# Stick-breaking attention: scores as two products over all 128 array rows, values padded to 128 columns

## The chip, the cores and the metric

One Trainium2 chip, one core of it. The metric is device time in microseconds (us) of one execution of the whole program; less is better. TensorE (PE in the profile) does the matmuls and loads their weights (PEld), VectorE is DVE, ScalarE is ACT, GpSimd is POOL, and SyncE (SP) issues the loads.

## The reference, cut to what matters

The program runs three transformer blocks in a row over 512 tokens of 1024 features. The change lies in the second one's mixer, stick-breaking attention with 16 heads of 64 dimensions:

```
z = einsum('bqhd,bkhd->bhqk', q_blk, k) * 64 ** -0.5
earlier = key_pos < q_pos
log_keep = where(earlier, log_sigmoid(-z), 0)
log_after = cumsum(log_keep over keys, reverse=True) - log_keep
weight = where(earlier, exp(log_sigmoid(z) + log_after), 0)
out = einsum('bhqk,bkhd->bqhd', weight, v)
```

The projections to q, k, v before it and the projection `w_out` after it belong to the same stage of the kernel. Everything is float32 in the reference. The kernel writes a float32 operand as the sum of a high part and a low part of a shorter type (F32R, `fp32r` in the profile) and adds products of parts: high by high, high by low and low by high.

## The kernel before, in words

`build` (L2064) runs the blocks one after the other: `block1`, `stick` (L601), `ffn`, `diff`, `ffn`. This change touches `stick` alone.

**Order.** `Driver` (L97) merges streams of work into one order of TensorE's instructions, by estimated microseconds (`mm`, L293, adds an estimate for each matmul) and by events that the streams set and wait for. The tile framework then orders the instructions of every engine by priority and by its own model of when operands are there. So a matmul stands in a fixed order in TensorE's queue, and a late operand holds what is behind it.

**Projections** (`projections`, L609). For each pair of heads `hp` (8 pairs) q and k are each one 128-feature chunk on all 512 tokens: 8 chunks of features by 3 products of parts, 24 matmuls of 512 columns. `evac_qk` (L610) multiplies the result by the norm's factor (DVE, L614), writes the high part on ACT (L615) and the low part on DVE (L616). Head 0 of the pair lies on partitions 0 to 63, head 1 on 64 to 127. For every second pair a group `g` of 256 columns of v (four heads) is projected with tokens on partitions; `scale_tm` (L571, L575) scales the result on ACT. The first pair and group are done side by side (`first_qk`, `first_v`), and their results wait for the norm's factors.

**Units** (`unit`, L664). One head's scores have keys on partitions and queries on columns, and only queries not before the key tile: key tile i has 512 - 128 i columns. They lie in three PSUM banks: tile 0, tile 1, and tiles 2 and 3 together. A unit is one bank of one head, so there are 48 units. Its steps: the score products and the mask into a bank `z` (5 banks); ACT does Abs, Exp and Ln (L686 to L688); DVE forms the softplus (L689) and splits it into `sh` and `sl` (L319, L320); TensorE adds the sums over later keys to the same bank, with the weights `negones` and `m_ntri`; ACT takes Exp into `w` (L705); TensorE multiplies `w` with v into the bank `po`, of which there is one. When both heads of a pair are through, `po` is split into `ohi` and `olo`, the operands of `w_out`.

The score products of one key tile take rows `d` of the array, the head's 64 partitions:

```
d = slice(64 * s, 64 * s + 64)
self.mm(zz, k[0][d, ks], q[0][d, P * i:], j == 0, False)
self.mm(zz, k[0][d, ks], q[1][d, P * i:], False, False)
self.mm(zz, k[1][d, ks], q[0][d, P * i:], False, False)
self.mm(zz[:, :P], self.neg30, self.m_ge, False, False)
```

The fourth, the mask, has all 128 rows and 128 columns. The product with v (L717) is in float32, not in parts; its weights are v's 64 columns of the head, and its output goes to the 64 partitions `d` of `po`. One float32 matmul stands in the trace as two records.

**Memory.** Tiles of 128 x 512 float32 come from one pool of 57 chunks (`big`), and scratch from a pool of 9 (`tmp`). A tile's place is free again after its last reader.

In the trace, `64*128` ahead of a matmul's shape means that its weights have 64 rows and 128 columns, and `128*64` that they have 128 rows and 64 columns.

Of the kernel before, what the change touches and what calls it, by code (L numbers as in the profile page):

```python
# [9 lines left out]
F32 = mybir.dt.float32  # L10
# [7 lines left out]
P = 128  # L18
T = 512
# [39 lines left out]
# 500000 ** (-j / 8) as float32 has it  # L59
# [5 lines left out]
def two_pi_parts():  # L65
    """2 pi as parts of 8, 12 and 24 bits"""
    rest, parts = 2 * math.pi, []
    for bits in (8, 12, 24):
        e = math.floor(math.log2(rest)) + 1 - bits
        part = math.floor(rest / 2.0 ** e) * 2.0 ** e if bits < 24 else rest  # L70
        parts.append(part)
        rest -= part
    return parts
# [11 lines left out]
class Slots:  # L85
    """free places of a resource, each with the time from which it is free"""
# [4 lines left out]
class Take:  # L91
    """n places of Slots at once"""
# [4 lines left out]
class Driver:  # L97
    """Merges the streams of work into one order of the tensor engine's instructions.

    A stream is a generator; it yields the microseconds until its next step's operands are there, an  # L100
    Event to wait for, or Slots of which it takes one."""
# [10 lines left out]
    def spawn(self, g):  # L112
        """one more stream, ahead of the others"""
        self.tasks.insert(0, [g, self.t, None])
# [38 lines left out]
class Raw:  # L153
    """x g of a norm as two parts, without the norm's factor 1/sqrt(mean of squares + eps) of the tokens; it
    goes on the results of the projections: r has it with the tokens on the free axis, rt on partitions"""
# [12 lines left out]
class Net:  # L168
    def __init__(self, ctx, tc, ins, out):
# [7 lines left out]
        # weights of the next proj_multi  # L177
# [3 lines left out]
        # the results of projections wait for this event  # L181
# [25 lines left out]
    def phase(self, name, **sizes):  # L207
        """pools of one part of the kernel"""
# [22 lines left out]
    def take(self, n):  # L231
        """counts n chunks as used"""
        self.mem.free.sort()
        del self.mem.free[:n]

    def drop(self, n, lat=0.0):
        """n chunks are read for the last time by what is issued now"""
        self.drv.release(self.mem, lat, n)
# [8 lines left out]
    def cmask(self, name, cmp, mult, base, val, dt=F32R):  # L247
        """val where base + mult*p + (-mult)*j  cmp 0, else 0"""
# [9 lines left out]
    def consts(self):  # L258
# [5 lines left out]
        # rows 0..63: 1, the others 0  # L264
# [7 lines left out]
        # [p, j]: 1 where p >= j, p <= j, p > j, p < j  # L272
# [4 lines left out]
        # columns 0..15 of the rows 16..31 of every 32  # L277
# [3 lines left out]
        # p - 32 b >= 16 and p - 32 b < 32, b by block of columns: one of the four is the row's own  # L281
# [40 lines left out]
    def wtile(self, ap, n=1024):  # L322
        """weights of one tile: [128, n] from DRAM, as two parts"""
# [11 lines left out]
    def wtile_big(self, ap):  # L335
        """weights [128, 1024] in chunks of 512 columns"""
# [12 lines left out]
    def evacuate(self, f, kind, lat, staged):  # L349
        """reads a bank, as soon as the norm's factors are there; a staged f only copies the bank, and returns the  # L350
        stream of the rest"""
# [12 lines left out]
    def proj_fm(self, w, h, evac, name, evs=None, lat=2.0, staged=False):  # L364
        """out[128 features, T] of one output chunk; w: (ap, k chunks) parts; evac(psum) reads the result"""
# [15 lines left out]
    def proj_tm(self, aps, h, evac, name, lat=2.0, evs=None, staged=False):  # L381
        """256 columns, tokens on partitions: evac(b, [128, 2 token tiles x 256]) for b = 0, 1"""
# [28 lines left out]
    def proj_halves(self, ap, h, evac, name):  # L411
        """the last output chunk before a norm, in two halves of the tokens: evac(psum, columns of the half)"""
# [12 lines left out]
    def proj_multi(self, items, h, name, evs, weights=None):  # L425
        """output chunks side by side, for operands that come slowly, with the weights in chunks of the big pool;
        items: (weights, evac(psum)) of a chunk of features, or ((weights, weights), evac(b, psum)) of 256 columns
        with tokens on partitions; at most 4 banks in all; the evacs are staged"""
# [35 lines left out]
    def out_proj(self, ws, h, evac, evs, late=1, last=None):  # L464
        """8 output chunks; the last `late` k chunks of the first two come after all their others"""
# [28 lines left out]
    def add_square(self, run, x):  # L494
        """run + x^2; run is None at the first"""
# [8 lines left out]
    def preload_ln(self):  # L504
        """the table of Ln and Exp, for the next norm"""
# [3 lines left out]
    def norm_sum(self, sums, cs):  # L509
        """sums over all features, on all partitions"""  # L510
# [5 lines left out]
    def rstd_of(self, sums, eps4=False, out=None, cs=slice(0, T), ps=None):  # L516
        """1/sqrt(mean of squares + eps) on all partitions, of the tokens cs; the squares' sums over the features of
        a partition are in sums, or ps has the sums over all"""
# [16 lines left out]
        # one Newton step: r (1.5 - 0.5 ms r^2)  # L535
# [35 lines left out]
    def scale_tm(self, out, ps, rt, b):  # L571
        """out = ps rt of the token tiles 2 b, 2 b + 1"""
# [19 lines left out]
    def add_to(self, x, R):  # L592
        """adds a projection to x; R, if any, takes the sum"""
# [7 lines left out]
    def stick(self, x, R, l, nxt, pre):  # L601
# [7 lines left out]
        def projections():  # L609
            def evac_qk(hp, wn, sc, ps):  # L610
                hi = self.chunk(wn + "hi", F32R)
                lo = self.chunk(wn + "lo", F32R)
                t = self.work("qk")
                nc.vector.tensor_tensor(t, ps, self.rfm, op=ALU.mult)  # L614
                nc.scalar.mul(hi, t, sc)  # L615
                nc.vector.scalar_tensor_tensor(out=lo, in0=t, scalar=sc, in1=hi.bitcast(F32),  # L616
                                               op0=ALU.mult, op1=ALU.subtract)
                qk[hp, wn] = (hi, lo)

            def evac_v(g, b, ps):  # L620
                t = v[g, b] = self.chunk(f"v{b}")
                self.scale_tm(t, ps, self.rt, b)
# [3 lines left out]
            def first_v(b, ps):  # L626
                t = v[0, b] = self.chunk(f"v{b}")
                nc.vector.tensor_copy(t, ps)

                def rest():  # L630
                    self.scale_tm(t, t, self.rt, b)
# [32 lines left out]
        def unit(hp, s, b, me, prev, head, pair):  # L664
            d = slice(64 * s, 64 * s + 64)
            # the key tiles of this bank: (tile, first column)
# [3 lines left out]
            hcol = 64 * ((2 * hp + s) % 4)  # L670
# [4 lines left out]
            q, k = qk[hp, "sb_q"], qk[hp, "sb_k"]  # L675
            z = self.bank("z", f"z{b}")
            for j, (i, c0) in enumerate(its):
                ks = slice(P * i, P * i + P)
                zz = z[:, c0:c0 + T - P * i]
                self.mm(zz, k[0][d, ks], q[0][d, P * i:], j == 0, False)  # L680
                self.mm(zz, k[0][d, ks], q[1][d, P * i:], False, False)
                self.mm(zz, k[1][d, ks], q[0][d, P * i:], False, False)
# [32 lines left out]
            for i, c0 in reversed(its):  # L715
                vt = v[g, i // 2][:, (i % 2) * 256 + hcol:(i % 2) * 256 + hcol + 64]
                self.mm(po[d, P * i:], vt, w[:, c0:c0 + T - P * i], i == 3, i == 0)  # L717
# [22 lines left out]
    def gates(self, R):  # L740
        """beta and the decays of the delta rule, tokens on partitions: columns (direction, chunk, head)"""
# [62 lines left out]
    def conv(self, ps, j, out, raw_h):  # L804
        """out = 2 silu(5-tap convolution along the tokens); ps: the channel's 512 tokens"""
# [18 lines left out]
    def silu2(self, out, ps, rt, b):  # L824
        """2 silu, without its factor rt"""
# [12 lines left out]
    def dn_prep(self, S, hh):  # L838
        """operands of one head of the batch S"""
# [6 lines left out]
        for x, w in enumerate("kq"):  # L846
            yield S["ev", w, hh]
            if w == "k":
                # kt, vt, U and two of aT
# [28 lines left out]
        # decays between the tokens of a chunk, both directions  # L878
# [35 lines left out]
        for w in "kq":  # L914
# [5 lines left out]
            if w == "k":  # L920
                # U of direction 0 is strictly upper, that of direction 1 strictly lower: one tile has both
# [17 lines left out]
    def dn_inv(self, S):  # L939
        """Y = (1 + U)^-1 of every head, direction and chunk of the batch: the diagonal blocks of 32 by  # L940
        substitution, one block per partition, then blocks of 64 and 128 on the tensor engine.
# [1222 lines left out]
```

## Time and profile before

| | |
|---|---|
| median of 3 runs | 2264.87 us |
| the three runs | 2253.7, 2264.87, 2268.81 us |
| span of the profiled execution, first to last instruction | 2268.6 us |
| PE busy | 2210.7 us (97%) |
| DVE busy | 1212.9 us (53%) |
| ACT busy | 963.9 us (42%) |
| POOL busy | 95.5 us (4%) |
| mean granted TensorE clock | 0.965 |

The profiled execution's own time is not listed apart from its span; the span is within 0.3 us of the slowest of the three runs. The stick-breaking stage lies between 907 and 1187 us of the span. "Busy" for PE means that a matmul was in the pipeline; it does not say how fast matmuls followed each other. The pace is read from the starts of successive matmuls in the timeline. The granted clock is 1.00 at the 2.4 GHz level and 0.50 at the 1.2 GHz level.

### The profile page before, as it was taken

To read this page: it belongs to the slowest core of one execution; us is meant where nothing else is said; L and a number is where in the kernel's file an instruction comes from. 1 tells how busy PE (TensorE), PEld (TensorE's weight loads), DVE (VectorE), ACT (ScalarE), POOL (GpSimd) and SP (SyncE) were. 2 spreads that over 40 slices of the span, in tenths; PEclk is the share of its full clock that TensorE was granted. 3 is DMA by queue.
4 is the path that set the end of the run, shared out by engine and by line. 5 is a ranking of instruction groups with operands and counts; after the bars stand their busy time and mean duration, and the time that the engine had idled before them with its cause. 6 is when DMAs were issued, how large, how long until landed. Compare 5 with 4: busy or idle time off the path is not lost.

```text
span 2268.6 us, 33416 instructions
## 1 busy us (share of the span) xinstructions
PE 2210.7 (97%) x13342; PEld 1855.4 (82%) x13342; DVE 1212.9 (53%) x2487; ACT 963.9 (42%) x1951; POOL 95.5 (4%) x109
## 2 busy tenths in 40 slices
PE   7999999989999998999999999999999999999999
PEld 6898898878888787777778888888999878888887
DVE  7865865976424567443346444433566656444421
ACT  5646666565423454544444223222444444232221
POOL 2000100000000000000000000000111100000000
PEclk9999999999999998899989999999898889999999
DMA  4221211323243521011103232233211113322332
GB/s 162 63 72 48 64 52 57 91 60 100 79 149 120 184 92 38 28 47 47 47 19 103 94 102 93 90 101 98 66 57 40 36 38 103 102 93 94 97 112 70
DMA packets 73995, 181.72 MB, mean 80 GB/s; under 512 B 24176, under 2 KB 24816, under 8 KB 73840
## 3 DMA queue, kind: packets, MB, share of 16 engines
q1 hardware_dynamic: 72560, 175.40, 24.2%
q0 software_dynamic: 1280, 4.20, 0.6%
q8 instruction: 105, 1.72, 0.3%
q14 instruction: 50, 0.41, 0.1%
HBM read 170.13 MB, written 9.44 MB: 79 GB/s over the span
## 4 chain that ended last, share of the span: by engine, by line
PE 84%; DVE 8%; ACT 3%; issue 1%; POOL 1%; DMA 1%; SPq 0%; DVEq 0%; ACTq 0%; POOLq 0%
PE pg L301 16%; PE pd L301 11%; PE pu L301 11%; PE po L301 9%; PE z L301 5%; PE pv L301 4%; PE pb L301 4%; PE s L301 3%; PE pz L301 2%; PE pq L301 2%; PE sb_q L301 2%; PE pk L301 2%; PE sb_k L301 2%; PE wS L301 2%; DVE cacc L818 1%
## 5 line engine op out<-in xcount | busy, mean ns | idle before, releaser
L317 ACT CAST whi<-st 128x1024 fp32r<-128x1024 f32 (+1 forms) x295 | 306.0, 1039 | 791.4 <-issue 340.3
L320 DVE TENSOR_TENSOR wlo<-st,whi 128x1024 fp32r<-128x1024 f32 (+1 forms) x295 | 355.9, 1208 | 284.8 <-ACT whi L317 280.9
L301 PE MATMUL pg<-rlo,whi 128*128 128x512 f32 x352 | 138.8, 394 | 0.0
L301 PE MATMUL pg<-rhi,whi 128*128 128x512 f32 x352 | 138.1, 392 | 0.0
L301 PE MATMUL pg<-rhi,wlo 128*128 128x512 f32 x352 | 138.0, 392 | 0.0
L301 PE MATMUL pd<-mh,whi 128*128 128x512 f32 x352 | 137.6, 391 | 0.0
L301 PE MATMUL pd<-mh,wlo 128*128 128x512 f32 x352 | 137.6, 391 | 0.0
L301 PE MATMUL pd<-ml,whi 128*128 128x512 f32 x352 | 137.5, 391 | 0.0
L301 PE MATMUL pu<-rhi,wlo 128*128 128x512 f32 x352 | 137.2, 390 | 0.0
L301 PE MATMUL pu<-rlo,whi 128*128 128x512 f32 x352 | 137.1, 390 | 0.0
L301 PE MATMUL pu<-rhi,whi 128*128 128x512 f32 x352 | 137.0, 389 | 0.0
L2032 DVE TENSOR_TENSOR sg<-pg,rfm 128x512 f32<-128x512 f32 x44 | 30.4, 691 | 118.5 <-PE pg L301 118.4
L2038 DVE TENSOR_TENSOR m<-pu,sg 128x512 f32<-128x512 f32 x44 | 30.4, 691 | 115.2 <-PE pu L301 115.2
L689 DVE SCALAR_TENSOR_TENSOR t<-z,t 128x384 f32<-128x384 f32 (+1 forms) x48 | 28.2, 600 | 99.8 <-ACT t L688 97.6
L301 PEld LDWEIGHTS pg<-rhi,wlo 128*128 128x128 f32 x352 | 66.2, 188 | 15.1 <-issue 0.5
L301 PEld LDWEIGHTS pg<-rlo,whi 128*128 128x128 f32 x352 | 66.3, 188 | 15.0 <-issue 0.5
L301 PEld LDWEIGHTS pg<-rhi,whi 128*128 128x128 f32 x352 | 66.2, 188 | 14.5
L301 PEld LDWEIGHTS pd<-ml,whi 128*128 128x128 f32 x352 | 66.2, 188 | 14.3
L301 PEld LDWEIGHTS pd<-mh,wlo 128*128 128x128 f32 x352 | 66.1, 188 | 14.3
L301 PEld LDWEIGHTS pd<-mh,whi 128*128 128x128 f32 x352 | 66.1, 188 | 14.2
L301 PEld LDWEIGHTS pu<-rhi,whi 128*128 128x128 f32 x352 | 66.1, 188 | 14.0
L301 PEld LDWEIGHTS pu<-rlo,whi 128*128 128x128 f32 x352 | 66.1, 188 | 14.0
(554 smaller groups left out, 5943.5 us busy)
## 6 DMA issues: line engine op xcount, KB each, us to landing
st<-w_gate SPq DMA_DIRECT2D x44, 512.0 KB, 3.4
st<-w_up SPq DMA_DIRECT2D x44, 512.0 KB, 3.4
st<-w_down SPq DMA_DIRECT2D x32, 512.0 KB, 3.5
st<-w_dn SPq DMA_DIRECT2D x24, 512.0 KB, 3.6
st<-w_out SPq DMA_DIRECT2D x24, 512.0 KB, 3.5
st<-w_down SPq DMA_DIRECT2D x16, 384.0 KB, 3.1
x<-xT SPq DMA_DIRECT2D x16, 256.0 KB, 5.9
st<-w_aq SPq DMA_DIRECT2D x8, 512.0 KB, 3.5
```

Source lines behind the costliest of these rows:

```text
L301: self.nc.tensor.matmul(out, lhsT=lhsT, rhs=rhs, start=start, stop=stop, skip_group_check=True)
L317: nc.scalar.copy(hi, src)
L320: nc.vector.tensor_tensor(lo, src, hi.bitcast(F32), op=ALU.subtract)
L689: nc.vector.scalar_tensor_tensor(out=t, in0=zz, scalar=0.0, in1=t, op0=ALU.max, op1=ALU.add)
L818: nc.vector.scalar_tensor_tensor(out=acc[:, a], in0=raw[:, b], scalar=w[:, s:s + 1], in1=acc[:, a], op0=ALU.mult, op1=ALU.add)
L2032: nc.vector.tensor_tensor(sg, ps, self.rfm, op=ALU.mult)
L2038: nc.vector.tensor_tensor(m, ps, sg, op=ALU.mult)
```

## The change

The score operands are stacked on partitions. For each head `stack` makes one query tile with the high part of q on the head's own 64 partitions and the low part on the other 64, and two key tiles: one with the high part of k on both halves, one with the low part of k on the own half and zeros on the other. Two products over 128 rows then give the three products of parts of before (the fourth term, of the zeros, adds nothing). The values are written with 64 columns of zeros beside each head's 64, so that the product with v has 128 columns of weights, writes all 128 partitions of `po`, and the two heads of a pair add up in one accumulation. Comments and docstrings are removed throughout; this is left out here.

```
+    def stack(self, box, j, query, src, sc):
+        nc = self.nc
+        for s in range(2):
+            own, other = slice(64 * s, 64 * s + 64), slice(64 - 64 * s, 128 - 64 * s)
+            f = sc if isinstance(sc, float) else sc[own]
+            x = src[own]
+            hi = self.chunk("qs" if query else "kh", F32R)
+            nc.scalar.mul(hi[own], x, f)
+            if query:
+                lo = hi[other]
+                box[j, "q", s] = hi
+            else:
+                t = self.chunk("kl", F32R)
+                nc.gpsimd.memset(t[other].bitcast(F32), 0.0)
+                lo = t[own]
+                box[j, "kh", s], box[j, "kl", s] = hi, t
+            nc.vector.scalar_tensor_tensor(out=lo, in0=x, scalar=f, in1=hi[own].bitcast(F32),
+                                           op0=ALU.mult, op1=ALU.subtract)
+            if not query:
+                nc.scalar.mul(hi[other], x, f)
...
             def evac_qk(hp, wn, sc, ps):
-                hi = self.chunk(wn + "hi", F32R)
-                lo = self.chunk(wn + "lo", F32R)
                 t = self.work("qk")
                 nc.vector.tensor_tensor(t, ps, self.rfm, op=ALU.mult)
-                nc.scalar.mul(hi, t, sc)
-                nc.vector.scalar_tensor_tensor(out=lo, in0=t, scalar=sc, in1=hi.bitcast(F32),
-                                               op0=ALU.mult, op1=ALU.subtract)
-                qk[hp, wn] = (hi, lo)
+                self.stack(qk, hp, wn == "sb_q", t, sc)
+
+            def pad_v(g, b, ps):
+                for i in range(2):
+                    t = v[g, 2 * b + i] = self.chunk(f"v{2 * b + i}")
+                    nc.gpsimd.memset(t.rearrange("p (a k) -> p a k", a=2)[:, :, 64:192], 0.0)
+                    nc.scalar.mul(t.rearrange("p (a k d) -> p a k d", a=2, k=4)[:, :, 0::3],
+                                  ps[:, i * 256:(i + 1) * 256].rearrange("p (a k d) -> p a k d", a=2, k=2),
+                                  self.rt[:, 2 * b + i:2 * b + i + 1])
 
             def evac_v(g, b, ps):
-                t = v[g, b] = self.chunk(f"v{b}")
-                self.scale_tm(t, ps, self.rt, b)
+                pad_v(g, b, ps)
...
             def first_v(b, ps):
-                t = v[0, b] = self.chunk(f"v{b}")
+                t = self.work(f"v{b}raw")
                 nc.vector.tensor_copy(t, ps)
...
-                    self.scale_tm(t, t, self.rt, b)
+                    pad_v(0, b, t)
...
-            hcol = 64 * ((2 * hp + s) % 4)
+            hcol = 128 * ((2 * hp + s) % 4)
...
-                self.mm(zz, k[0][d, ks], q[0][d, P * i:], j == 0, False)
-                self.mm(zz, k[0][d, ks], q[1][d, P * i:], False, False)
-                self.mm(zz, k[1][d, ks], q[0][d, P * i:], False, False)
+                self.mm(zz, kh[:, ks], q[:, P * i:], j == 0, False)
+                self.mm(zz, kl[:, ks], q[:, P * i:], False, False)
                 self.mm(zz[:, :P], self.neg30, self.m_ge, False, False)
...
-                vt = v[g, i // 2][:, (i % 2) * 256 + hcol:(i % 2) * 256 + hcol + 64]
-                self.mm(po[d, P * i:], vt, w[:, c0:c0 + T - P * i], i == 3, i == 0)
+                self.mm(po[:, P * i:], v[g, i][:, hcol:hcol + P], w[:, c0:c0 + T - P * i], s == 0 and i == 3, s == 1 and i == 0)
```

## Rows read from the trace of the kernel before

**Rows 1.** The page: busy us, share of the span and instructions by engine.
```profile
PE 2210.7 (97%) x13342; PEld 1855.4 (82%) x13342; DVE 1212.9 (53%) x2487; ACT 963.9 (42%) x1951; POOL 95.5 (4%) x109
```

**Rows 2.** Windows: stretch, length, busy us (instructions) by engine, clock, DMA share, GB/s.
```profile
907.00:1187.00 280.00, 280.00 (x1331) 211.53 (x1331) 116.19 (x197) 129.43 (x243) 0.00 (x0) 0.90 0.12 38
126.00:355.00 229.00, 221.69 (x2413) 202.50 (x2413) 145.88 (x376) 137.43 (x377) 14.40 (x12) 1.00 0.20 59
1645.00:1861.00 216.00, 215.19 (x1371) 189.16 (x1370) 132.59 (x465) 93.44 (x203) 26.73 (x19) 0.86 0.14 45
```

**Rows 3.** Timeline, one head's scores: start us, duration us, engine, line, operation, shapes.
```profile
976.61 0.39 PE L301 MATMUL sb_q<-rhi,wlo 128*128 128x512 f32 x1
976.92 0.38 PE L301 MATMUL z<-sb_qhi,sb_khi 64*128 64x256 f32 x1
...
977.26 0.27 PE L301 MATMUL z<-sb_qhi,sb_klo 64*128 64x256 f32 x1
977.47 0.33 PE L301 MATMUL z<-m_ge,neg 128*128 128x128 f32 x1
977.73 0.33 PE L301 MATMUL z<-sb_qhi,sb_khi 64*128 64x128 f32 x1
...
980.58 0.38 PE L301 MATMUL z<-sb_qhi,sb_khi 64*128 64x256 f32 x1
```

**Rows 4.** Timeline, the sums over later keys of one bank: full-array matmuls.
```profile
958.81 0.22 PE L301 MATMUL z<-sh,negones 128*128 128x128 f32 x1
958.87 0.28 PE L301 MATMUL z<-sl,negones 128*128 128x128 f32 x1
958.98 0.33 PE L301 MATMUL z<-sh,negones 128*128 128x256 f32 x1
...
960.07 0.28 PE L301 MATMUL pv<-whi,rhi 128*128 128x256 f32 x1
```

**Rows 5.** Timeline of the first block: a mask product with the same weights.
```profile
73.83 0.39 PE L301 MATMUL dec<-m_gt,neg 128*128 128x512 f32 x1
74.06 0.40 PE L301 MATMUL dk<-hlo,whi 128*128 128x512 f32 x1
```

**Rows 6.** Timeline: one product with v between projection matmuls.
```profile
961.62 0.40 PE L301 MATMUL sb_q<-rhi,wlo 128*128 128x512 f32 x1
961.94 1.07 PE L301 MATMUL po<-w,v 128*64 128x512 f32 x2
...
963.29 0.39 PE L301 MATMUL sb_q<-rlo,whi 128*128 128x512 f32 x1
```

**Rows 7.** Timeline: a float32 matmul of the full array between projection matmuls.
```profile
1226.78 1.10 PE L301 MATMUL nsum<-sq,ones 128*128 128x512 f32 x2
...
1227.94 0.39 PE L301 MATMUL pg<-rhi,wlo 128*128 128x512 f32 x1
```

**Rows 8.** Timeline: the first two of one pair's three runs with v, merged.
```profile
990.21 2.37 PE L301 MATMUL po<-w,v 128*64 128x128 f32 x8
...
995.36 1.51 PE L301 MATMUL po<-w,v 128*64 128x128 f32 x6
```

**Rows 9.** Windows: the stretch before a fall of the clock, and the stretch after.
```profile
979.20:982.60 3.40, 3.40 (x17) 2.49 (x16) 2.02 (x5) 3.40 (x8) 0.00 (x0) 1.00 0.00 0
...
982.70:986.10 3.40, 3.40 (x10) 2.58 (x9) 3.12 (x7) 2.15 (x6) 0.00 (x0) 0.50 0.00 0
```

**Rows 10.** Timeline at the lower clock: two successive projection matmuls.
```profile
983.75 0.63 PE L301 MATMUL sb_q<-rlo,whi 128*128 128x512 f32 x1
984.18 0.63 PE L301 MATMUL sb_q<-rhi,wlo 128*128 128x512 f32 x1
```

**Rows 11.** Groups by form: ACT and DVE in the stage, POOL in the span.
```profile
L615 ACT ACTIVATE sb_khi<-qk 128x512 fp32r<-128x512 f32 x8 | 5.0, 628 | 1.7 <-DVE qk L614 1.7
...
L616 DVE SCALAR_TENSOR_TENSOR sb_klo<-qk,sb_khi 128x512 fp32r<-128x512 f32 x8 | 5.5, 685 | 0.1
...
L1418 POOL MEMSET Y<- 128x512 f32 x4 | 1.9, 530 | 0.0
```

More of the change, by code (lines that the diff above doesn't have):

```diff
@@ L664, in unit @@
         def unit(hp, s, b, me, prev, head, pair):
-            d = slice(64 * s, 64 * s + 64)
             its = ((2, 0), (3, 256)) if b == 2 else ((b, 0),)
@@ L674, in unit @@
             yield self.free["z"]
-            q, k = qk[hp, "sb_q"], qk[hp, "sb_k"]
+            q, kh, kl = qk[hp, "q", s], qk[hp, "kh", s], qk[hp, "kl", s]
             z = self.bank("z", f"z{b}")
```

## The prediction

> **What bounds the kernel now.** I read the page first: TensorE is busy 97% of the span, VectorE 53%, ScalarE 42% [rows 1]. The windows view then gives the stage of the change, 907 to 1187 us [rows 2]: TensorE busy 280.00 of 280.00 us, ScalarE 129.43, VectorE 116.19, GpSimd nothing. So the stage lasts as long as TensorE's queue takes, and two things set that: how closely matmuls follow each other (starts in the timeline) and the granted clock. The clock's mean here is 0.90; in the first block's attention, whose products use the full array, it is 1.00, and in the differential attention, whose score products have 64 rows as here, 0.86 [rows 2].
>
> **Score products.** One head's scores are 12 products of 64 rows and 4 masks of 128 rows. They run from 976.92 to 980.58, 3.66 us at full clock [rows 3]. The columns alone do not explain it: the product ahead of a mask keeps the engine 0.21 us (977.26 to 977.47) for 256 columns, and the mask 0.26 us (977.47 to 977.73) for 128. That is a cost of the change of shape, paid twice per key tile. After the change everything here has 128 rows. A row for it exists: the sums over later keys of one bank are eight full-array matmuls of twice 128, 256, 384 and 512 columns, exactly the count and widths of one head's products after the change, and take 958.81 to 960.07, 1.26 us [rows 4]. A mask of 128 columns at full shape should take what 128 columns take there, 958.87 to 958.98, 0.11 us; and a mask with the same weights between full-array matmuls shows no extra, 0.23 us for 512 columns [rows 5]. Sum: 1.26 + 4 x 0.11 = 1.70 us. Saved: 1.96 us a head, **31.4 us** over 16 heads. Entering such a burst costs the matmul ahead 0.31 instead of 0.23 us (976.61 to 976.92 [rows 3]); at two bursts a pair, 16 x 0.08 = **1.3 us** more.
>
> **Product with v.** The pair of records at 961.94 stands between projection matmuls that otherwise follow every 0.23 us. From 961.62 + 0.23 to 963.29 - 0.23 it costs 1.21 us [rows 6]. A float32 matmul of the full array, also 512 columns and with 128 columns of weights to load, costs 1227.94 - 0.23 - 1226.78 = 0.93 us [rows 7]. So the padding itself costs nothing that shows, and a run of such products saves 0.28 us. A pair has three such runs in the timeline, of 8 and 6 records [rows 8] and one of 2 as in [rows 6]: 24 x 0.28 = **6.7 us**.
>
> **Clock.** Within the stage the clock falls eight times to 0.50, the 1.2 GHz level. What comes before is the same each time: a stretch of score products and masks (in one of the eight shared with products with v), with TensorE busy throughout (3.40 of 3.40 us) and still at 1.00, the 2.4 GHz level; then 0.50 [rows 9]. At that level a projection matmul of 512 columns takes 0.43 us instead of 0.23 [rows 10]. A mean of 0.90 over 280 us is 56 us at the lower level, which cost 56 x (1 - 0.23 / 0.43) = **26 us**. The first block's attention has the same pattern of three products, masks and float32 products with v, on full rows, and holds 1.00 for 229 us [rows 2]. So I take all 26 us as gained. The Trainium skill, TensorE: Matmul & The Clock Gate (Part 1), says that the gate follows how busy the engine has been. By busy time alone these falls should not occur, and full rows should not end them; the trace disagrees as long as "busy" means the PE row. With it the sum below would be 31 us and not 57, and the rule returns as a rival.
>
> **What is added.** Each pair's q and k cost ScalarE six scalings instead of two: 4 x 0.63 = 2.5 us a pair; VectorE four low parts instead of two: 2 x 0.69 = 1.4 us [rows 11]. No row has these forms on 64 partitions; I take them at the durations of 128, with the same 512 columns. Over 8 pairs that is 20 and 11 us. ScalarE then has about 149 us and VectorE 127 in a stage of some 215: 70% and 59%. Beneath: nothing, because ScalarE is idle 151 of these 280 us and VectorE 164 [rows 2]. Above: all 31 us on the path. I take 1 us a pair, **8 us**, near the lower end: TensorE has the next pair's projections between the steps of a pair, but the scores now come in about half the time, so ScalarE's three activations per bank are more often what is last. The first head of a pair needs one scaling and one low part for q and for k, as before; the second head's come while the first's products run.
>
> GpSimd gets 32 memsets, 16 of 64 x 512 and 16 of 128 x 256, at most 0.53 us each [rows 11], 17 us on an engine idle in this stage; behind them in its queue stands only the next norm's small power. A memset waits only for a free chunk, and the low part of k follows it. Cost nothing while a chunk is free ahead of the projection's end; without that cover, 0.53 us per memset. The scaling of v has the same count and width, with a strided output; nothing. The first v's raw copy moves from a chunk to scratch: nothing, since both are ready before the norm's factors. No DMA is added, removed or moved.
>
> **Sum.** 31.4 + 1.3 + 6.7 + 26 - 8 = 57 us. Against the profiled span: 2268.6 - 57 = 2211.6. The median of the runs stands 3.7 us below that span, so the forecast is 2264.87 - 57 = 2208, call it **2209 us**. Own range: all of the 65 us and the lowest run, 2253.7 - 65 = 2189, to 2222 with twice the stalls and a fall or two of the clock left.
>
> **Rivals.**
> (a) The clock still falls: the low activity comes from short matmuls and masks, or from something the half rows only go along with. For it: TensorE is already busy all through each stretch before a fall [rows 9], so "busy" does not explain them. Against: the first block [rows 2]. Time: 2209 + 26 = 2235. By the skill's rule named above, busy time would decide and this is what follows.
> (b) ScalarE and VectorE become the bound: all 31 us of their additions lie on the path instead of 8. For it: 70% of a stage with bursts. Against: 151 us of ScalarE's idle time to use up [rows 2]. Time: 2209 + 23 = 2232.
> (c) The delay belongs to the mask product, not to the change of shape: then only one product in three goes, 1.26 / 2 x 16 = 10 us instead of 33. Against: the mask in [rows 5]. Time: 2209 + 23 = 2232, and no more than one percent if (a) comes with it.
> (d) Slower: chunks run out. A pair's stacks are 6 chunks instead of 4, a group's values 4 instead of 2. Counted at the fifth finished pair with two pairs' stacks, two groups' values and both heads' sums alive: before 16 (the norm's output) + 8 + 4 + 12 + 10 (outputs) = 50 of 57; after 16 + 12 + 8 + 12 + 10 = 58, one too many. Then the next pair's q and k (48 matmuls x 0.23 = 11 us) have nowhere to go and no longer fill TensorE's time between the steps, which lie bare instead. It decides if it strikes more than 57 / 11, about 5 of the 7 later pairs; at all seven the time is 2209 + 77 = 2286, with the clock falling in the waits 2286 + 26 = 2312. Against: the maxima do not fall together; values of the older group end with the pair that the count has finishing, and one chunk too few is a short wait.
>
> **Chances.** Forecast 0.70, (a) 0.12, (b) 0.08, (c) 0.05, (d) 0.05. About 1%, 23 us, is what a measurement of this kernel can tell from no change: below 2242 is faster, above 2288 slower. Faster: 0.70 + 0.10 of (a) + 0.06 of (b) + 0.03 of (c) = 0.89; same: 0.07, where two of (a), (b), (c) meet; slower: 0.04, most of (d). The range runs from 2189 to 2243: it takes in the lone cases (a), (b), (c) and leaves out their meetings and (d).
>
> **What would show it.** Right: products of one head with their masks take about 1.7 us in the timeline, all `128*128`; the mask 0.11 us; the clock in the stage 0.98 or more; the stage some 57 us shorter; PE still busy over 97% of it. The stages before and after keep their length within a few us. Wrong: falls to 0.50 in the stage (a); PE idle with ACT as the releaser (b); masks still at 0.26 us (c); PE or POOL idle ahead of memsets or q and k evacuations, with projections bunched after a pair's last product with v (d).

## The result and the profile after

The changed kernel takes 2211.66 us, the median of 4 runs (2205.83 to 2215.02), against 2266.84 us for the kernel before, also 4 runs (2253.70 to 2274.84). The ratio is 0.9748, with a 95% interval from 0.9707 to 0.9789: faster by about 55 us. Forecast were 2209 us and a range of 2189 to 2243.

The page of the kernel after, busy time by engine and the granted clock in 40 slices of the span:
```profile
span 2213.2 us, 33421 instructions
...
PE 2152.9 (97%) x13278; PEld 1835.6 (83%) x13278; DVE 1222.8 (55%) x2503; ACT 980.7 (44%) x1983; POOL 108.9 (5%) x141
...
PEclk9999999999999998999999999999889889999999
```
Beside [rows 1]: TensorE still has 97%, of a span 55.4 us shorter; ScalarE and VectorE are busy 17 and 10 us longer, GpSimd 13. The page can't say where the 55 us were. For that I cut both traces at the same instructions: the stage runs from the first float32 sum of squares (`nsum`) of its norm to that of the next norm. The columns are those of [rows 2].

Windows of the kernel before: ahead of the stage, the stage, and from there to the last block's norm.
```profile
0.00:897.46 897.46, 845.68 (x6704) 737.42 (x6705) 575.16 (x1290) 475.57 (x1156) 59.19 (x83) 0.98 0.28 90
...
897.46:1226.78 329.32, 328.99 (x1541) 250.21 (x1540) 148.97 (x241) 154.42 (x280) 1.03 (x1) 0.92 0.14 44
...
1226.78:1905.64 678.86, 676.88 (x3532) 572.81 (x3531) 347.41 (x793) 242.42 (x405) 35.33 (x25) 0.94 0.24 76
```
The same windows of the kernel after:
```profile
0.00:904.32 904.32, 852.12 (x6705) 743.52 (x6705) 575.26 (x1290) 475.75 (x1156) 60.60 (x87) 0.97 0.28 90
...
904.32:1175.82 271.50, 269.18 (x1476) 227.30 (x1476) 158.67 (x257) 171.05 (x312) 12.99 (x29) 1.00 0.17 53
...
1175.82:1850.29 674.47, 672.47 (x3531) 569.76 (x3531) 347.50 (x793) 242.35 (x405) 35.33 (x25) 0.95 0.24 77
```
The stage went from 329.32 to 271.50 us, **57.8 us** less, and its clock from 0.92 (54.6 us of it at 0.50) to 1.00 (none). The stretch ahead, which the change does not touch, is 6.9 us longer at a lower clock (0.98, then 0.97), and the one behind 4.4 us shorter at a higher one; the rest is equal. 57.8 - 6.9 + 4.4 = 55.3 us, the difference of the spans. The 6.9 us are no cost of the change: in the kernels below, whose work ahead of the stage is the same, this stretch ends anywhere from 898.6 to 904.2 us.

Timeline of the kernel after, one head's scores (columns as in [rows 3]):
```profile
970.46 0.39 PE L301 MATMUL sb_q<-rhi,wlo 128*128 128x512 f32 x1
970.68 0.28 PE L301 MATMUL z<-qs,kh 128*128 128x256 f32 x1
970.80 0.28 PE L301 MATMUL z<-qs,kl 128*128 128x256 f32 x1
970.92 0.22 PE L301 MATMUL z<-m_ge,neg 128*128 128x128 f32 x1
970.98 0.27 PE L301 MATMUL z<-qs,kh 128*128 128x128 f32 x1
...
972.35 0.33 PE L301 MATMUL z<-qs,kh 128*128 128x256 f32 x1
...
1015.33 0.28 PE L301 MATMUL pv<-wlo,rhi 128*128 128x256 f32 x1
1015.45 1.02 PE L301 MATMUL po<-w,v 128*128 128x512 f32 x2
1015.91 0.79 PE L301 MATMUL sb_q<-rhi,whi 128*128 128x512 f32 x1
1016.54 0.39 PE L301 MATMUL sb_q<-rlo,whi 128*128 128x512 f32 x1
```
The head runs from 970.68 to 972.35, 1.67 us instead of 3.66 [rows 3]. The mask at 970.92 keeps the engine 0.06 us, and the product ahead of it 0.12, where before they kept it 0.26 and 0.21; the burst costs the matmul ahead of it 0.22 us, no more than any projection. The product with v at 1015.45 takes, to the second projection behind it less 0.23, 0.86 us instead of 1.21 [rows 6].

### The profile page after: what moved, and what is told of

Its sections match the earlier page's. It is cut to its first block, busy times and chain, and to the rows that moved or that the text cites. A ratio compares the mean times of both kernels' runs of the same rounds, so it can differ in the third digit from the quotient of the medians.

```text
span 2213.2 us, 33421 instructions
## 1 busy us (share of the span) xinstructions
PE 2152.9 (97%) x13278; PEld 1835.6 (83%) x13278; DVE 1222.8 (55%) x2503; ACT 980.7 (44%) x1983; POOL 108.9 (5%) x141
## 4 chain that ended last, share of the span: by engine, by line
PE 83%; DVE 9%; ACT 4%; issue 2%; POOL 1%; DMA 1%; SPq 0%; DVEq 0%; ACTq 0%; POOLq 0%
PE pg L301 17%; PE pd L301 11%; PE pu L301 11%; PE po L301 9%; PE pb L301 4%; PE pv L301 4%; PE s L301 3%; PE pz L301 3%; PE z L301 3%; PE pq L301 2%; PE pk L301 2%; PE wS L301 2%; PE sb_q L301 2%; DVE cacc L845 1%; PE sb_k L301 1%
## 5 line engine op out<-in xcount | busy, mean ns | idle before, releaser
L301 PE MATMUL pz<-wlo,hhi 128*128 128x256 f32 x256 | 75.2, 294 | 3.3 <-DVE wlo L320 2.5
```

The source lines that it names most:

```text
L301: self.nc.tensor.matmul(out, lhsT=lhsT, rhs=rhs, start=start, stop=stop, skip_group_check=True)
```

## The experiments

Each is an edit of one of the two kernels. "Stage" is the stretch between the two `nsum` records, "low" the time in it at a granted clock of 0.50. Ratios are to the kernel before, run on the same chip at the same time. The stage of e8 and e10 is that of the kernel after, unchanged: its three traces agree within 0.01 us.

| kernel | stage, us | low, us | ratio (95%) |
|---|---|---|---|
| before | 329.3 | 54.6 | |
| after | 271.5 | 0 | 0.9748 (0.9707 to 0.9789) |
| e1 scores only | 280.4 | 0 | 0.9801 (0.9773 to 0.9829) |
| e2 values only | 316.4 | 37.5 | 0.9940 (0.9911 to 0.9970) |
| e3 three full-row products | 279.2 | 0 | 0.9777 (0.9747 to 0.9807) |
| e4 before, no mask | 279.1 | 0 | 0.9763 (0.9732 to 0.9795) |
| e5 after, float32 mask | 278.3 | 0 | 0.9803 (0.9769 to 0.9837) |
| e6 the same in two halves | 296.6 | 0 | 0.9858 (0.9823 to 0.9893) |
| e7 ScalarE's additions doubled | 291.8 | 6.8 | 0.9852 (0.9817 to 0.9888) |
| e9 copy of k on GpSimd | 272.5 | 0 | 0.9755 (0.9716 to 0.9794) |
| e11 before, no mask, one half | 283.6 | 0 | 0.9804 (0.9739 to 0.9870) |
| e8 stack in `diff` too | 271.5 | 0 | 0.9613 (0.9580 to 0.9645) |
| e10 e8, later due time | 271.5 | 0 | 0.9619 (0.9565 to 0.9672) |

**e1: the scores alone** (v and the product with v as before).
```
-                self.mm(po[:, P * i:], v[g, i][:, hcol:hcol + P], w[...], s == 0 and i == 3, s == 1 and i == 0)
+                vt = v[g, i // 2][:, (i % 2) * 256 + hcol:(i % 2) * 256 + hcol + 64]
+                self.mm(po[d, P * i:], vt, w[...], i == 3, i == 0)
```


> Only the score half of the change: scores as two stacked products over 128 rows, values and their product with the weights as before (128 x 64). The stage is measured from one norm's sums to the next (before: 897.46 to 1226.78, 329.3 us; changed kernel: 904.32 to 1175.82, 271.5 us). My theory (the gain is the change of shape, the third product and the clock; the values are a small part): about 50 us of the 58 us, a stage of 278 to 281 us, no fall of the clock in the stage, time about 2218. Rival (the products with v at half columns are what makes the clock fall, or the two halves only work together): falls remain, and the stage stays above 295 us.

Window of the stage:
```profile
899.11:1179.55 280.44, 277.86 (x1476) 219.01 (x1476) 157.94 (x257) 171.72 (x312) 9.36 (x17) 1.00 0.15 52
```
48.9 of the 57.8 us come with the scores, every fall of the clock among them; the padded values add 8.9 on top.

**e2: the values alone** (q, k and the scores as before).
```
-                self.mm(zz, kh[:, ks], q[:, P * i:], j == 0, False)
-                self.mm(zz, kl[:, ks], q[:, P * i:], False, False)
+                self.mm(zz, k[0][d, ks], q[0][d, P * i:], j == 0, False)
+                self.mm(zz, k[0][d, ks], q[1][d, P * i:], False, False)
+                self.mm(zz, k[1][d, ks], q[0][d, P * i:], False, False)
```


> Only the value half: values padded to 128 columns, scores as three products of 64 rows as before. My theory: 24 runs save 0.28 us each, 7 us, and the clock still falls about eight times in the stage: stage about 322 us, time about 2259. Rival (the clock falls because of the products with v at 64 columns): no falls, a further 25 us, stage below 300 us.

```profile
904.16:1220.51 316.35, 315.88 (x1541) 251.90 (x1540) 149.35 (x241) 154.97 (x280) 4.49 (x13) 0.94 0.13 46
```
13.0 us were gained, not 7. Seven falls are left, 37.5 us at 0.50 instead of 54.6. The 17.1 us fewer are worth 17.1 x (1 - 0.23 / 0.43) = 8 us, which leaves 5 us of pace. Half-row scores with masks keep the falls alive, then. That the values make them fewer is not shown: each kernel has one trace here, e2's is of the slowest of its ten runs (2267.2 us, median 2249.7), and in the differential attention, which only e8 and e10 touch, the low time of the other eleven traces lies anywhere from 47.8 to 81.9 us.

**e3: three products over full rows** (k's tiles zero on the other head's partitions, so nothing is stacked).
```
-                self.mm(zz, kh[:, ks], q[:, P * i:], j == 0, False)
-                self.mm(zz, kl[:, ks], q[:, P * i:], False, False)
+                self.mm(zz, kh[:, ks], q[0][:, P * i:], j == 0, False)
+                self.mm(zz, kh[:, ks], q[1][:, P * i:], False, False)
+                self.mm(zz, kl[:, ks], q[0][:, P * i:], False, False)
```


> The changed kernel, but with three score products of 128 rows: high and low parts of q of both heads as they come, and per head the high and the low part of k with zeros on the other head's 64 rows. So the shape is that of the changed kernel and the number of products that of the one before; half of the weights are zeros. My theory (shape sets pace and clock): one product more per key tile, 16 x 0.63 = 10 us above the changed kernel, a stage of 281 to 283 us and no fall of the clock. Rival (the gain is the third product that goes): stage above 300 us. Rival on the clock (it goes by what is in the array, not by the shape): falls as before, stage about 307 us.

```profile
899.54:1178.74 279.20, 277.94 (x1540) 236.72 (x1540) 153.32 (x249) 156.80 (x288) 18.78 (x41) 1.00 0.15 52
```
With as many matmuls as before the stage is already 50.1 of the 57.8 us shorter; that is what the uniform shape of scores and values is worth. The last 7.7 us, where 10 were expected, are the third product less what the stacking adds elsewhere: e3 has one of the four added scalings a pair (ScalarE is busy 156.8 us, in the kernel after 171.1).

**e4: the kernel before without its masks**, half rows kept.
```
-                self.mm(zz[:, :P], self.neg30, self.m_ge, False, False)
```


> The kernel before without its mask products: the scores of later keys are not masked. The three score products of a key tile keep 64 rows and now follow each other with no change of shape between them. By the paces shown, a head takes 1.5 x 1.26 = 1.9 us instead of 3.66, 28 us less over 16 heads. Theory one (rows in use alone make the clock fall): eight falls remain, stage about 300 us. Theory two (it takes the standing still at each change of shape as well): the clock stays at 1.00, stage about 275 us. I hold the first a little likelier, since the differential attention shows the same falls.

```profile
904.22:1183.30 279.08, 277.37 (x1477) 215.41 (x1476) 146.78 (x241) 150.88 (x280) 1.03 (x1) 1.00 0.15 52
```
This one went against me. I held that half rows make the clock fall, and expected falls; there was none, and the stage came down to 279 us. Timeline of this kernel, where the first head's products end:
```profile
971.90 0.33 PE L301 MATMUL z<-sb_qlo,sb_khi 64*128 64x384 f32 x1
972.08 0.33 PE L301 MATMUL z<-sb_qhi,sb_klo 64*128 64x384 f32 x1
972.08 0.56 PE L301 MATMUL z<-sb_qhi,sb_khi 64*128 64x256 f32 x2
972.31 0.28 PE L301 MATMUL z<-sb_qlo,sb_khi 64*128 64x256 f32 x1
972.42 0.28 PE L301 MATMUL z<-sb_qhi,sb_klo 64*128 64x256 f32 x1
972.48 0.39 PE L301 MATMUL z<-sb_qlo,sb_khi 64*128 64x512 f32 x1
972.55 0.22 PE L301 MATMUL z<-sb_qhi,sb_khi 64*128 64x128 f32 x1
```
At 972.08 two products start together, and from there products of 256 and 512 columns start 0.06 to 0.23 us apart: the second head's, on the other 64 rows, run beside the first head's. The Trainium skill, TensorE: Matmul & The Clock Gate (Part 3), says that matmuls on different row groups of the array run at the same time; the trace agrees, with 16 score products that start 2 to 8 ns after one of the other head. Before the change a 128-row mask stood after every third product and shut this out, but for one such start. So e4 left two explanations for the steady clock: no change of shape, or two heads at once. e11 tells them apart.

**e11: e4 with both heads on partitions 0 to 63**, so that nothing can run side by side (head 1 thus takes head 0's operands).
```
-                self.mm(zz, k[0][d, ks], q[0][d, P * i:], j == 0, False)
+                self.mm(zz, k[0][dz, ks], q[0][dz, P * i:], j == 0, False)
...
```


> The kernel before without its mask products, and with both heads of a pair computed from the first head's q and k, on partitions 0 to 63 (the second head's scores are left out). In the earlier run without masks the second head's products started 3 to 6 ns after some of the first head's, so the two halves of the array were in use at once and that run could not show what half rows alone do. Here that is excluded. Half rows alone make the clock fall: falls to 0.50 in most pairs, stage above 295 us. Half rows alone do not: the clock stays at 1.00, and the stage is that of the earlier run (279.1 us) plus what the overlap saved, up to 0.5 us a pair, 280 to 285 us. I now hold the second likelier.

```profile
903.05:1186.64 283.59, 282.36 (x1477) 220.22 (x1476) 146.83 (x241) 151.44 (x280) 1.03 (x1) 1.00 0.15 51
```
Timeline, from the first head's last tile to the second head's first product:
```profile
972.15 0.39 PE L301 MATMUL z<-sb_qhi,sb_khi 64*128 64x512 f32 x1
972.38 0.39 PE L301 MATMUL z<-sb_qlo,sb_khi 64*128 64x512 f32 x1
972.61 0.39 PE L301 MATMUL z<-sb_qhi,sb_klo 64*128 64x512 f32 x1
972.85 0.27 PE L301 MATMUL z<-sb_qhi,sb_khi 64*128 64x256 f32 x1
```
Every product waits for the one ahead, 0.23 us per 512 columns, and the clock still stays at 1.00. Half rows alone, one head at a time, do not make it fall. One of the four timed runs, at 7006 us, is left out of the ratio.

**e5 and e6: the mask in float32, whole (e5), and as two products of 64 weight columns (e6)**, on the kernel after. e6 puts the change of shape back while every product keeps 128 rows.
```
-                self.mm(zz[:, :P], self.neg30, self.m_ge, False, False)
+                for y in (slice(0, 64), slice(64, 128)):
+                    self.mm(z[y, c0:c0 + P], self.neg30.bitcast(F32)[:, y], self.m_ge.bitcast(F32), False, False)
```


> The changed kernel with the mask product in float32 instead of the short type, full array: two records of 0.11 us and the float32 overhead of about 0.08 us in place of 0.06 us. It is the control for the next run. Both theories: no fall of the clock in the stage, 64 x 0.24 = 15 us more than the changed kernel's 271.5 us, a stage of about 287 us, time about 2227.

> The changed kernel with each mask as two float32 products of 128 rows and 64 columns (the upper and the lower half of the keys), so that full-row score products again alternate with another shape, as before the change, but no product has 64 rows. Pace alone: 64 x (4 records of 0.12 + 0.3 for the two changes of shape) against 64 x 0.3 in the control, some 30 us more than the control, a stage of about 317 us. Theory two (standing still at changes of shape is enough for the clock to fall): falls to 0.50 in most pairs, a further 10 to 25 us, 327 us or more. Theory one (it takes half rows as well): the clock stays at 1.00, about 317 us.

Window of e5:
```profile
900.88:1179.17 278.29, 276.33 (x1541) 234.07 (x1540) 159.02 (x257) 170.88 (x312) 12.74 (x29) 1.00 0.15 52
```
Window of e6:
```profile
903.04:1199.66 296.62, 295.87 (x1668) 233.15 (x1668) 160.05 (x257) 172.72 (x312) 12.73 (x29) 1.00 0.14 49
```
Timeline of e6, one head:
```profile
976.09 0.28 PE L301 MATMUL z<-qs,kh 128*128 128x256 f32 x1
976.20 0.28 PE L301 MATMUL z<-qs,kl 128*128 128x256 f32 x1
976.41 0.44 PE L301 MATMUL z<-m_ge,neg 128*64 128x128 f32 x4
976.78 0.33 PE L301 MATMUL z<-qs,kh 128*128 128x128 f32 x1
...
979.47 0.39 PE L301 MATMUL z<-qs,kh 128*128 128x256 f32 x1
```
The float32 mask costs 278.3 - 271.5 = 6.8 us, 0.11 us a tile, where I had expected 15; the mask in halves 296.6 - 278.3 = 18.3 us more over 64 key tiles, 0.29 us a tile, where I had expected 30. In the 0.29 us are both changes of shape and two more records a tile, each of which starts 6 to 7 ns after its partner. The product ahead of a mask now keeps the engine 0.21 us (976.20 to 976.41) instead of 0.12, as before the change. A head is nearly as slow as before (3.38 us against 3.66), and yet the clock stays at 1.00: standing still at changes of shape is not enough either.

**e7: each of ScalarE's scalings of q and k written twice**, to see how much room the change left it.
```
             nc.scalar.mul(hi[own], x, f)
+            nc.scalar.mul(hi[own], x, f)
...
                 nc.scalar.mul(hi[other], x, f)
+                nc.scalar.mul(hi[other], x, f)
```


> The changed kernel with every scaling on ScalarE in the stacks written twice (6 more of 0.63 us a pair, 30 us in all). My theory (ScalarE's additions are covered by TensorE's work but for the first and the last pair): stage 272 to 276 us, time 2 us above the changed kernel. Rival (ScalarE has become the bound, what was called (b)): 20 us or more above it.

```profile
904.22:1195.98 291.76, 278.89 (x1476) 230.47 (x1476) 157.82 (x257) 199.82 (x360) 12.81 (x29) 0.99 0.14 50
```
Waits of TensorE in that stage (idle us, times, longest):
```profile
PE z L301 <- ACT kh L626: 5.5, 9, 0.7
```
I expected 2 us and got 20.3. ScalarE is busy 69% of the stage, no bound by its share, but 29 us more of it took 20 us: TensorE idles 12.9 us, 5.5 of them before a head's first product, which waits for the second half of `kh` (six second heads and three first ones), and the clock is low for 6.8 us. The change stands close to this edge, which its 63% does not show.

**e9: that second half of `kh` copied by GpSimd**, which takes two of the four added scalings per pair off ScalarE.
```
-                nc.scalar.mul(hi[other], x, f)
+                nc.gpsimd.tensor_copy(hi[other], hi[own])
```


> The changed kernel with the second copy of k's high part made by GpSimd instead of ScalarE: ScalarE's additions fall from four to two scalings a pair (10 us less over 8 pairs). The run before it showed that 30 us more on ScalarE cost 20 us of the stage, against my expectation of 2. If the additions of the change itself are paid at that rate, the stage falls by 6 to 7 us, to about 265 us. If they are covered up to about their present size and only what goes beyond is paid, it stays at 270 to 272 us. A copy on GpSimd that is slower than 1.5 us could make the second head of a pair late: then above 272 us with TensorE waiting for POOL.

```profile
902.24:1174.74 272.50, 269.36 (x1477) 227.23 (x1476) 163.41 (x257) 162.10 (x296) 28.93 (x45) 1.00 0.15 53
```
ScalarE is busy 9 us less, and the stage is 1.0 us longer. These scalings were covered, then. GpSimd's copy takes 1.02 us where ScalarE's scaling takes 0.63, and TensorE waits 1.1 us for it in all.

**e8: the same stacking in the differential attention**, the other stage with half-row scores and a low clock (0.86 in [rows 2]); **e10** adds a later due time for its results.
```
-            hi = self.chunk(w + "hi", F32R)
-            lo = self.chunk(w + "lo", F32R)
-            nc.scalar.mul(hi, ps, gv)
...
+            self.stack(fm, j, w == "q", ps, gv)
...
-                self.mm(zz, q[0][d, qs], k[0][d, :n], True, False)
-                self.mm(zz, q[1][d, qs], k[0][d, :n], False, False)
-                self.mm(zz, q[0][d, qs], k[1][d, :n], False, False)
+                self.mm(zz, q[:, qs], kh[:, :n], True, False)
+                self.mm(zz, q[:, qs], kl[:, :n], False, False)
```
```
-DF_LAT5 = 4.0
+DF_LAT5 = 6.5
```


> The changed kernel with the same stacking of q and k in the differential attention, where each score product also has 64 rows and alternates with a mask of 128 rows. In the changed kernel's trace the clock is at 0.50 for some 65 us there. My theory (same mechanism, same paces): 16 x 1.96 = 31 us from the pace and 65 x 0.46 = 30 us from the clock, less some 10 us for the memsets on GpSimd ahead of its small powers and the longer evacuation; 2160 to 2170, clearly faster than both kernels. Rival (that stage is bound by its chain on VectorE, ScalarE and GpSimd, and the clock falls in waits): less than 20 us, falls remain.

> The kernel with both attentions stacked, and the planner's due time for the normed output of a head of the differential attention (DF_LAT5) raised from 4.0 to 6.5 us. TensorE stood still five times for 1.5 to 2.5 us there, with VectorE's scaling of that output as the releaser. If the order is the cause, some 8 to 10 us come back: 2172 us, the stretch from the third norm's sums to the last at 635 us instead of 644. If VectorE is simply behind (it is busy 73% there), the waits move to other instructions and the time stays within 3 us of 2181.

Window of e8, from `nsum` to the last block's `nsum`:
```profile
1172.51:1816.51 644.00, 626.06 (x3468) 543.93 (x3467) 356.26 (x809) 261.38 (x437) 43.75 (x41) 0.98 0.24 81
```
The same of e10:
```profile
1170.05:1811.33 641.28, 623.73 (x3467) 541.10 (x3467) 356.52 (x809) 262.59 (x437) 44.85 (x41) 0.99 0.24 81
```
The low clock in that stretch falls from 64.9 to 20.5 us and the stretch from 674.5 to 644.0, 30 us and not the 50 I expected, since TensorE now idles 17.9 us in it. Waits of TensorE in e8, 1500 to 1830 us:
```profile
PE otr L305 <- DVE os L2007: 10.4, 5, 2.5
```
The faster scores leave VectorE late with the heads' results. The later due time moved these waits (17.6 us idle) and took 2.7 us from the stretch, close to what was expected if VectorE is simply behind. At 2181.6 us (e8) and 2177.5 us (e10) both beat the changed kernel; their ratios are too close to call between them.

## Why the prediction was right

**What bounds it.** TensorE's queue before, and after too: 269.2 of 271.5 us busy. The stage shortened by 57.8 us where 57 were forecast. The mechanisms were the right ones, the clock's in part; that the sum is so close is in part luck, because the gains were put some 5 us too high and the losses as much too high.

**Pace of the scores.** Forecast 1.70 us a head, measured 1.67: (3.66 - 1.67) x 16 = 31.8 us against 31.4, entries 16 x (0.31 - 0.22) = 1.4 against 1.3. That the delay belongs to the change of shape and not to half rows or to the mask product is shown from three sides, the clock's share included: e3 (full rows, three products) keeps 50 us of the gain, e11 (half rows, no mask, no overlap) 46, and e6 (full rows, shape changed for the mask) loses 18 to its control. The Trainium skill, TensorEngine Tiling (Array Packing), Key Properties, says that a change of tiling mode drains TensorE; the trace agrees in that the product ahead of a change keeps the engine 0.21 us instead of 0.12. e6 puts the pair of changes around a mask at 0.29 us, its two more records included.

**Product with v.** Forecast 24 x 0.28 = 6.7 us. One run saves 1.21 - 0.86 = 0.35 us: [rows 7], the float32 matmul I took as model, keeps 0.07 us more than the padded product does. But the number of runs was wrong too. In the kernel after, seven of the eight pairs have four runs with v where there were three [rows 8], 31 in all instead of 24. Timeline of the kernel after, the runs of one pair:
```profile
979.73 2.32 PE L301 MATMUL po<-w,v 128*128 128x128 f32 x8
...
983.91 0.87 PE L301 MATMUL po<-w,v 128*128 128x128 f32 x4
...
985.32 0.81 PE L301 MATMUL po<-w,v 128*128 128x384 f32 x2
...
992.08 1.02 PE L301 MATMUL po<-w,v 128*128 128x512 f32 x2
```
e1 has the same 31 runs, so its 8.9 us are the padding's worth in the new order. Against the kernel before, the products with v became only 5.8 us shorter.

**Clock.** Forecast: all falls go, 26 us. They went: 54.6 us of low clock, 54.6 x (1 - 0.23 / 0.43) = 25 us (23.7 if each record is compared with its own kind at 1.00). The size was nearly right and the cause only half told. I named the half rows by comparing with the first block [rows 2]; the runs show a conjunction. With TensorE's row full the clock falls in this stage where 64-row products alternate with 128-row ones (before, e2), and not where either is missing: half rows without masks (e4, e11), shape changes with full rows (e6). (e7's one fall, 6.8 us, comes behind waits of 1.2 and 1.8 us.) The differential attention fits: e8 took 44 of the 65 us of low clock out of its stretch, and what is left there lies at waits of 1.5 to 2.5 us. Two limits of this: e6 changes the number of weight columns, not of rows, and no run alternates half and full rows without the delay. So it stays open whether the alternation itself counts, or only that half rows and lost time come together. As for busy time, TensorE's row is full before each fall [rows 9] as it is nearly all through e11 (282.4 of 283.6 us), which has none, so the row cannot have decided; rival (a) is out for this change.

**Additions to ScalarE and VectorE.** Forecast 8 us lost, 1 us in every pair. About 3 are found, and not in every pair: TensorE's idle time in the stage is 2.3 us (0.3 before), six waits of note, two in the first pair and four in or behind the last. Timeline of the kernel after, two of them with the record ahead of each:
```profile
922.76 0.40 PE L301 MATMUL z<-sh,m_ntri 128*128 128x512 f32 x1
923.80 0.49 PE L301 MATMUL z<-sl,m_ntri 128*128 128x512 f32 x1 [0.64 <-DVE sl L320]
...
1135.21 1.02 PE L301 MATMUL po<-w,v 128*128 128x512 f32 x2
1136.90 0.72 PE L301 MATMUL po<-ohi,whi 128*128 128x512 f32 x2 [0.67 <-ACT ohi L317]
```
By starts the first costs 1.04 - 0.23 = 0.81 us and the second 1.69 - 0.86 = 0.83. The other four cost 0.4 to 0.5 each, and one of them was there before. They lie where no projections are left to fill with. e9 speaks against the scalings as a price of every pair, and so does e3, which has one of the four added ones and still 1.2 us of idle time.

**The sum.** One head and one run, multiplied, would give 31.8 + 1.4 + 8.4 + 25 = 67 us of gains. Added up over every start in the stage of both traces (a record at 0.50 counted at what its kind took at 1.00, the rest put down to the clock; what a burst costs its neighbours counted with the burst), scores and masks gave 30.8 us, the products with v 5.8 and the clock 23.7. That is 60.3 us, where 65.4 were forecast; 2.0 us of idle time and 0.5 us in other matmuls go off, which leaves 57.8. So two misses of some 5 us, the gains and the additions, cancelled each other.

**Rivals (b) to (d).** (b): ScalarE is at 63% and holds little up, though e7 shows how near it is. (c): the mask takes 0.06 to 0.11 us. (d): projections still stand between the bursts, and TensorE has no idle time of the size. GpSimd's memsets, by groups from 880 to 1140 us of the kernel after, take what [rows 11] gave:
```profile
L618 POOL MEMSET kl<- 64x512 f32 x16 | 8.6, 535 | 69.2 <-PE z L301 29.1 <-PE po L301 29.0 <-issue 5.8
```
GpSimd itself waits for chunks that TensorE frees (`z`, `po`), as (d) assumed, and it is in time.

## What to carry to other kernels

Look in the timeline for short matmuls of one array shape between longer ones of another: the busy row shows 100% there, and starts that lie further apart than the columns ask for are the loss. Either give all of them one shape, at the price of zeros, or, where the program can do without it, take the odd one out, which leaves half-row products of two heads free to run side by side (e4 shows the time; it leaves the scores of later keys unmasked). Then look again at the engines that feed the shortened stretch: their share of busy time says little about how much more they can bear.

## What was not expected of the hardware

- The clock fell to 0.50 with TensorE's row full, and only where half-row and full-row matmuls alternated: 54.6 us in the stage before, none in e4, e6 and e11. In all thirteen traces, a fall behind a full row stands in this stage of the kernel before and of e2, or in the differential attention where its scores have 64 rows.
- Two halves of the array ran side by side as soon as no full-row mask stood between them: 16 such starts of score products in e4, one in the kernel before. Without that overlap (e11) the stage took 4.5 us more. That e4 and e3 end at 279.1 and 279.2 us says nothing on half against full rows, since e4 has no masks and e3 has padded values.
- Half the partitions save no time on ScalarE or VectorE. Groups of the kernel after, 880 to 1140 us (the same operations on 128 partitions took 628 and 685 ns [rows 11]):
```profile
L612 ACT ACTIVATE kh<-qk 64x512 fp32r<-64x512 f32 x16 | 10.1, 628 | 4.4 <-DVE qk L638 4.3
...
L621 DVE SCALAR_TENSOR_TENSOR kl<-qk,kh 64x512 fp32r<-64x512 f32 x16 | 10.9, 684 | 4.2 <-ACT kh L612 4.0
```
